# A decoder step on one core: where the first squares are made, how x and the last products are cut, and the order of the streams

## The chip, the core and the metric

The kernel runs on one NeuronCore of a Trainium2 chip. The metric is the time of one execution on the device in microseconds (us). The engines are named as in the profile: PE multiplies matrices, DVE works on vectors, ACT on scalars and activations, POOL (GpSimd) and SP (SyncE) mostly issue transfers. Each engine takes its instructions in order, and semaphores order them across engines.

## The reference

One step of a one-layer decoder with two token mixers, on 256 prompt tokens and 8 x 8 sample tokens (T = 320 columns, D = 1024). Branch A is block-sparse softmax attention with rotary queries and keys, branch B is stick-breaking attention; both read a cache of 1024 past tokens for each of the 8 samples through a page table. All is float32.

```
def decoder_layer(x, pos_start, past, w):
    h = rms_norm(x, g_mix)
    proj = einsum('btd,de->bte', h, w_in)        # q, k, v of A; q, k, v of B; two gates
    qa, ka = rope(qa, pos), rope(ka, pos)
    new_rows = (ka, va, ks, vs)                  # also outputs
    o_a = moba_block(qa, past and new keys, values)
    o_s = stick_breaking_block(qs, past and new keys, values)
    merged = (sigmoid(ga) * einsum('btw,wd->btd', o_a, w_branch_moba)
              + sigmoid(gs) * einsum('btw,wd->btd', o_s, w_branch_sb))
    x = x + einsum('btd,de->bte', merged, w_out)
    h2 = rms_norm(x, g_ffn)
    ff = silu(einsum('btd,df->btf', h2, w_ffn_gate)) * einsum('btd,df->btf', h2, w_ffn_up)
    return x + einsum('btf,fd->btd', ff, w_ffn_down), new_rows
# prompt: no past; sample: past = cache[page_table]; then y = rms_norm(x, g_final)
```

## The kernel before

Activations lie with D on the 128 partitions (8 pieces) and the 320 tokens as columns. Every matrix product is made of three: both factors are split into a high part that PE takes in its fast 32-bit form and a low part, the rest; high by high, low by high and high by low are added in one PSUM tile. A weight tile (128 x 1024, 512 KB) so costs a load on SP's queue into one of three raw buffers `wr`, a copy on ACT (`wh`), a subtraction on DVE (`wl`), both into one of three pairs of buffers, and 24 matmuls of 320 columns.

The head (`load_x`) loads x in quarters of two pieces and the first two weights in halves, makes the high and low parts `xs` and `xl` piece by piece, and squares x for the first norm: four ACT instructions of two pieces each into `sq`, and on DVE two folds and a last add. `rsqrt` then sums over the partitions with six short matmuls (`cs`) after the third dense tile, ACT and DVE turn this into `rtok`, and `first_norm` spreads it to `rstd` with the matmuls `rb` after the fourth.

The attention part interleaves six streams: dense tiles (`d`: queries and keys, values, later the branch products), scores of sample pairs against cached keys (`s`), transposed probabilities and cached values (`a`), prompt attention (`p`), ends (`e`), gates (`g`). The string `ORDER` of 113 letters gives the order of their steps; `Plan.run` takes one step for each letter and then calls `loads.feed`. A pair's scores and its values both come in two halves, and each half takes two tiles of 1 MB from a ring of 8 buffers `cr`. So the first pair (branch 0, samples 0 and 1) has the letters s s, then a a a: probabilities, first half of the values, second half.

`loads.feed` starts loads in the order of need, with at most one cache tile for each call, as long as buffers are free. Keys (`kr`) and weights go out on SP's one queue in that order. Values (`vr`) are gathered by POOL; ahead of each gather POOL copies one element of the second last key tile (`seen`), so that a gather starts only when that key tile has landed. PE, POOL and SP keep the order in which the program is written; the other engines are ordered by a scheduler after the head.

After that come the output projection, the feed-forward part and the down projection, whose PE work is dense, and `last_norm`: PE sums the squares, ACT and DVE make `r`, and the eight pieces are multiplied by it and stored, six by DVE one at a time and the last two by POOL.

## Time and profile before

| | |
|---|---|
| median of 3 runs | 558.27 us (555.37 to 559.37) |
| profiled execution | 559.79 us, its span 558.0 us |
| mean granted clock of PE | 0.993 |
| PE | 542.0 us busy, 97% of the span |
| DVE, ACT, POOL | 329.7, 269.9, 49.8 us busy |
| DMA | 138.86 MB, mean 249 GB/s |

The span is the profiled execution from its first to its last instruction. All rows below come from this one execution, so sums are made against its 559.79 us. The page divides the span into 40 slices of 14 us; PE shows 8 or 9 tenths in each but the last.

### The profile page before, as it was taken

The numbers are of one execution on the slowest core, as the hardware profiler recorded it, in microseconds if no ns is written. First come the engines' busy times: TensorE is split into PE (matmuls) and PEld (weight loads), VectorE is DVE, ScalarE is ACT, GpSimd is POOL, SyncE is SP. The second block draws the span as 40 slices with busy tenths as digits, with TensorE's granted clock in tenths as the row PEclk, the third lists the DMA queues.
The fourth block names the chain that finished last, engine by engine and source line by source line (L and its number), as shares of the span: only waits on it lengthen the run. The fifth ranks groups of instructions, "written<-read, shape, count | busy, mean of one in ns | idle before, by whom it ended". The sixth has DMA issues, their size and how long they took to land.

```text
span 558.0 us, 10927 instructions
## 1 busy us (share of the span) xinstructions
PE 542.0 (97%) x4252; PEld 493.2 (88%) x4252; DVE 329.7 (59%) x600; ACT 269.9 (48%) x484; POOL 49.8 (9%) x73
## 2 busy tenths in 40 slices
PE   8999999999999999999999999999999999999993
PEld 5888676878878678878999999999999999999992
DVE  5786655464468537763778666555556665443433
ACT  6895555436675436542445464444333333353421
POOL 0001212150034302130000000000000000000001
PEclk9899999999999999999999999999999999999998
DMA  6999999999799999995595544544445454545512
GB/s 218 369 395 395 337 378 401 401 408 403 256 348 362 419 392 333 388 373 208 171 331 158 149 148 150 150 149 151 146 147 149 144 155 134 155 145 143 169 34 94
DMA packets 45572, 138.86 MB, mean 249 GB/s; under 512 B 5201, under 2 KB 7505, under 8 KB 41297
## 3 DMA queue, kind: packets, MB, share of 16 engines
q1 hardware_dynamic: 40336, 104.06, 54.8%
q0 software_dynamic: 4608, 33.56, 14.8%
q8 instruction: 33, 0.54, 0.4%
q10 hardware_dynamic: 576, 0.56, 0.3%
q14 instruction: 19, 0.15, 0.1%
HBM read 134.22 MB, written 3.93 MB: 248 GB/s over the span
## 4 chain that ended last, share of the span: by engine, by line
PE 82%; DMA 9%; DVE 3%; ACT 2%; SPq 1%; issue 1%; POOL 1%; DVEq 0%; POOLq 0%; ACTq 0%
PE dps L185 55%; PE dps L344 15%; PE po L696 4%; DMA vr<-in_cv,small 4%; DMA kr<-in_ck 3%; PE S L571 3%; DMA wr<-in_w_in 1%; DVE wl L153 1%; SPq L533 1%; PE tp L504 1%; PE tp L672 1%; PE dps L518 1%; PE dps L388 1%; PE dps L463 1%; DMA small<-in_c_small 1%
## 5 line engine op out<-in xcount | busy, mean ns | idle before, releaser
L152 ACT ACTIVATE wh<-wr 128x1024 fp32r<-128x1024 f32 (+1 forms) x122 | 127.2, 1046 | 179.5 <-issue 104.5
L153 DVE TENSOR_TENSOR wl<-wr,wh 128x1024 fp32r<-128x1024 f32 (+1 forms) x122 | 147.0, 1206 | 67.9 <-ACT wh L152 66.9
L185 PE MATMUL dps<-x1h,wh 128*128 128x320 f32 x352 | 109.0, 310 | 0.0
L185 PE MATMUL dps<-x1l,wh 128*128 128x320 f32 x352 | 108.8, 309 | 0.0
L185 PE MATMUL dps<-x1h,wl 128*128 128x320 f32 x352 | 108.8, 309 | 0.0
L344 PE MATMUL dps<-xs,wh 128*128 128x320 f32 x256 | 78.8, 320 | 0.9 <-ACT xs L306 0.9
L344 PE MATMUL dps<-xl,wh 128*128 128x320 f32 x256 | 77.2, 314 | 0.3 <-DVE xl L307 0.3
L185 PEld LDWEIGHTS dps<-x1h,wh 128*128 128x128 f32 x352 | 66.1, 188 | 0.1
L185 PEld LDWEIGHTS dps<-x1l,wh 128*128 128x128 f32 x352 | 66.1, 188 | 0.0
L185 PEld LDWEIGHTS dps<-x1h,wl 128*128 128x128 f32 x352 | 66.1, 188 | 0.0
L185 PE MATMUL dps<-fh,wh 128*128 128x320 f32 x176 | 54.4, 309 | 0.0
L185 PE MATMUL dps<-fl,wh 128*128 128x320 f32 x176 | 54.4, 309 | 0.0
L185 PE MATMUL dps<-fh,wl 128*128 128x320 f32 x176 | 54.4, 309 | 0.0
L344 PEld LDWEIGHTS dps<-xs,wh 128*128 128x128 f32 x256 | 48.8, 191 | 4.7 <-issue 2.0
L344 PEld LDWEIGHTS dps<-xl,wh 128*128 128x128 f32 x256 | 48.9, 191 | 1.1 <-DVE xl L307 1.0
L344 PE MATMUL dps<-xs,wl 128*128 128x320 f32 x256 | 43.2, 309 | 0.0
L344 PEld LDWEIGHTS dps<-xs,wl 128*128 128x128 f32 x256 | 39.1, 188 | 0.2 <-DVE wl L312 0.2
L541 POOL DMA_INDIRECT vr<-in_cv,small x32 | 35.9, 1121 | 19.1 <-PE po L696 8.6
L696 PE MATMUL po<-vr,pt 128*32 128x256 f32 x512 | 32.1, 381 | 2.9 <-DMA vr<-in_cv,small 2.9
L185 PEld LDWEIGHTS dps<-fh,wh 128*128 128x128 f32 x176 | 33.0, 188 | 0.0
L185 PEld LDWEIGHTS dps<-fl,wh 128*128 128x128 f32 x176 | 33.0, 188 | 0.0
L185 PEld LDWEIGHTS dps<-fh,wl 128*128 128x128 f32 x176 | 33.0, 188 | 0.0
(203 smaller groups left out, 844.6 us busy)
## 6 DMA issues: line engine op xcount, KB each, us to landing
kr<-in_ck SPq DMA_DIRECT2D x128, 256.0 KB
wr<-in_w_ff SPq DMA_DIRECT2D x44, 512.0 KB
wr<-in_w_in SPq DMA_DIRECT2D x30, 512.0 KB
wr<-in_w_down SPq DMA_DIRECT2D x16, 448.0 KB
wr<-in_w_v SPq DMA_DIRECT2D x8, 512.0 KB
wr<-in_w_b SPq DMA_DIRECT2D x8, 512.0 KB
wr<-in_w_out SPq DMA_DIRECT2D x8, 512.0 KB
wr<-in_w_down SPq DMA_DIRECT2D x8, 512.0 KB
```

What stands on the lines that cost most here:

```text
L152: self.nc.scalar.activation(hi, raw, AF.Copy)
L153: self.nc.vector.tensor_tensor(lo, raw, r32(hi), ALU.subtract)
L185: nc.tensor.matmul(ps, w, x, start=first and i == 0, stop=last and i == len(todo) - 1)
L344: self.nc.tensor.matmul(ps, a, x, start=k + low + i == 0, stop=low == 1 and k + n == KD and i == n - 1)
L388: nc.tensor.matmul(ps, self.xs[:, k], w[k][j], start=k + j == 0, stop=k + j == KD)
L463: nc.tensor.matmul(S[e][:, i], q[r, 2 * u + i, half * P:half * P + P], k[r, 2 * u + i, half * P:NP_], start=True, stop=True)
L504: nc.tensor.transpose(tp[:, i * P:(i + 1) * P], src, self.ident)
L518: nc.tensor.matmul(po[r, i, :NP_ if kt else P], t["v"][:, kt, c0:c0 + HD], mv, start=kt == 1, stop=kt == 0)
L533: nc.sync.dma_start(raw[:, g], ck[bass.ds(at[g] * P, P), :])
L541: self.nc.gpsimd.indirect_dma_start(out=raw.rearrange("p a b -> p (a b)"), out_offset=None, in_=self.I[f"cv{br}"], in_offset=bass.Indirect ...
L571: nc.tensor.matmul(S[r], self.block(QS, x, hp), raw[x][:, :, hp * P:(hp + 1) * P], start=i == 0, stop=i == 1)
L696: nc.tensor.matmul(po[r], PT[j][:, r], v[:, c:c + 256], start=j == 0, stop=j == 8)
```

## The change

Five things change.

First squares: the first two pieces of x are squared right behind the second piece's high part, inside the loop over pieces, and the other three squares follow in a loop that adds each result on DVE at once, 640 columns at a time, where there was one add of 1280 and one of 640.

x lies in memory as four contiguous quarters, and the later reload of x for the residual is four transfers.

The last products: pieces 0 and 1 alone as before, then the last two on POOL, then 2 and 3, and 4 and 5, together on DVE; five stores in place of seven, on SP, ACT, ACT, SP, SP.

`ORDER` and `FIRST` have new letters: the second half of the first pair's values comes ahead of the third pair's first scores, the two halves of values of several pairs stand side by side, and gates move. `feed` counts with a variable that equals `self.ready` for `WLAG = 0`. `queries` of the second branch's first pair are made one step group earlier.

```
@@ -36,7 +36,9 @@
 
 LAG = 2
 PACE = 1
-FIRST = "wwwwc"
+
+WLAG = 0
+FIRST = "wwwcww"
 ORDERED = {mybir.EngineType.PE, mybir.EngineType.Pool, mybir.EngineType.SP}
 STARTED = ORDERED | {mybir.EngineType.DVE, mybir.EngineType.Activation}
 WR, WB = 3, 3
@@ -50,8 +52,8 @@
 
 
 ORDER = (
-    "dddddddsdddsdddsdaspaddsadasegaddaapedsapdpsggdaapepaaddgpds"
-    "spepdgddpsagasapggegapaapgpsseggpggpdsagdasaaedgaaded"
+    "dddddddsdddsdddsdasaddpasadsedpdgaaadspdpseggdaaapegpaaddpds"
+    "spepddgdpsaggsaapggegapaappsseggpggpdsagdasaaedgaaded"
 )
 
 
@@ -94,14 +96,17 @@
 
     def feed(self):
 
+        ready = self.ready
         while self.raw and self.ready - self.used["w"] < WB:
             self.split_one()
+        if not WLAG:
+            ready = self.ready
         left, held, begun = [], set(), 0
         for kind, load in self.todo:
             if kind == "c":
                 free = self.begun["c"] - self.used["c"] < RB and begun < PACE
             else:
-                free = self.begun["w"] - self.ready < WR
+                free = self.begun["w"] - ready < WR
             if free and kind not in held:
                 tile = load()
                 (self.raw if kind == "w" else self.got["c"]).append(tile)
@@ -289,7 +294,7 @@
         w = [self.wpool.tile([P, 1024], F32, name=self.uid("wr"), tag="wr", bufs=WR) for i in range(2)]
         parts = [self.weight_parts() for i in range(2)]
         load_w = lambda i, h: nc.sync.dma_start(w[i][:, half[h]], self.I["w_in"][i][:, 4 * h:4 * h + 4])
-        load_x = lambda g: nc.sync.dma_start(x[:, 2 * g:2 * g + 2], self.I["x"][:, 2 * g:2 * g + 2])
+        load_x = lambda g: nc.sync.dma_start(x[:, 2 * g:2 * g + 2], self.I["x"][g])
         nc.scalar.dma_start(self.small, self.I["c_small"])
         for h in range(2):
             load_x(2 * h)
@@ -310,13 +315,14 @@
             if k % 4 == 1:
                 for (hi, lo), raw in zip(parts, w):
                     nc.vector.tensor_tensor(lo[:, half[h]], raw[:, half[h]], r32(hi[:, half[h]]), ALU.subtract)
+            if k == 1:
+                nc.scalar.activation(sq[:, 0:2], x[:, 0:2], AF.Square)
         self.loads.are_split(parts)
         self.loads.split_one()
-        for k in range(0, KD, 2):
+        for k in range(2, KD, 2):
             nc.scalar.activation(sq[:, k:k + 2], x[:, k:k + 2], AF.Square)
+            nc.vector.tensor_add(sq[:, :2], sq[:, :2], sq[:, k:k + 2])
         nc.scalar.activation(self.xs[:, :, NS:], r32(self.xl[:, :, NP_:]), AF.Copy)
-        for n in (4, 2):
-            nc.vector.tensor_add(sq[:, :n], sq[:, :n], sq[:, n:2 * n])
         self.sq = self.stg.tile([P, T], F32, name="sq", tag="y", bufs=3)
         nc.vector.tensor_add(self.sq, sq[:, 0], sq[:, 1])
 
@@ -418,10 +424,11 @@
                 self.first_norm()
             while todo:
                 self.qk_tile(br, *todo.pop(0))
-            if f == HP - 1:
+            if f % 8 == HP - 1:
 
                 for u in range(2):
-                    self.queries(br, u)
+                    if br == 0 or f"s0{u + 2}" in self.plan.done:
+                        self.queries(br, u)
 
     def gen_v(self, br):
         for c in range(2):
@@ -765,7 +772,8 @@
         self.x1h = xh = q.tile([P, KD, T], F32R, name="x1h")
         self.x1l = xl = q.tile([P, KD, T], F32R, name="x1l")
         self.rstd2 = rstd = q.tile([P, T], F32, name="rstd2")
-        nc.sync.dma_start(x1, I["x"])
+        for g in range(4):
+            nc.sync.dma_start(x1[:, 2 * g:2 * g + 2], I["x"][g])
         acc = self.acc1 = q.tile([P, 1, T], F32, name="acc1")
         def part(e, k0, k1):
             w, ps = made[e]
@@ -856,13 +864,11 @@
 
         rb = self.pp.tile([P, T], F32, name="rstd3", tag="s", bufs=SB)
         nc.scalar.activation(rb, r, AF.Copy)
-        e = 0
-        for i, n in enumerate((1, 1, 1, 1, 1, 1, 2)):
-            s = slice(e, e + n)
-            engine, v = (nc.gpsimd, r) if i == 6 else (nc.vector, rb if i else r)
-            engine.tensor_tensor(x1[:, s], xg[:, s], v[:, None, :].to_broadcast([P, n, T]), ALU.mult)
-            (nc.scalar if i % 2 else nc.sync).dma_start(self.O["y"][:, s], x1[:, s])
-            e += n
+        tiles = (nc.vector, nc.sync, 0, 1), (nc.vector, nc.scalar, 1, 2), (nc.gpsimd, nc.scalar, 6, 8), (nc.vector, nc.sync, 2, 4), (nc.vector, nc.sync, 4, 6)
+        for engine, queue, e0, e1 in tiles:
+            v = r if engine is nc.gpsimd or e0 == 0 else rb
+            engine.tensor_tensor(x1[:, e0:e1], xg[:, e0:e1], v[:, None, :].to_broadcast([P, e1 - e0, T]), ALU.mult)
+            queue.dma_start(self.O["y"][:, e0:e1], x1[:, e0:e1])
 
     def needs(self):
 
@@ -967,7 +973,7 @@
     f = lambda x: np.ascontiguousarray(x)
     xp, xs = np.asarray(i["x_prompt"]), np.asarray(i["x_sample"])
     x = np.concatenate([xp[0, ::-1], xs[:, ::-1].reshape(NS, D)])
-    a["x"] = f(x.T.reshape(KD, P, T).transpose(1, 0, 2))
+    a["x"] = f(x.T.reshape(4, 2, P, T).transpose(0, 2, 1, 3))
 
     def tiles(w, k, n):
         return f(np.asarray(w).reshape(k, P, n, P).transpose(2, 1, 0, 3))
```

The order of instructions, first on ACT at the head, before (`sq` are the squares, `wh_151` and `wh_258` the high parts of the third and fourth weight):

```order
L309 ACTIVATE wh_111<-wr_108 128x512
L306 ACTIVATE xs<-x_105,small 128x320 x3
L309 ACTIVATE wh_109<-wr_107 128x512
L306 ACTIVATE xs<-x_105,small 128x320
L309 ACTIVATE wh_111<-wr_108 128x512
L306 ACTIVATE xs<-x_105,small 128x320 x2
L152 ACTIVATE wh_151<-wr_122 128x1024
L316 ACTIVATE sq_106<-x_105 128x640 x4
L317 ACTIVATE xs<-xl 128x8x64
L152 ACTIVATE wh_258<-wr_124 128x1024
```

The squares stand together there, ahead of `wh_258`. After, on ACT at the same place:

```order
L314 ACTIVATE wh_111<-wr_108 128x512
L319 ACTIVATE sq_106<-x_105 128x640
L311 ACTIVATE xs<-x_105,small 128x320 x3
L314 ACTIVATE wh_109<-wr_107 128x512
L311 ACTIVATE xs<-x_105,small 128x320
L314 ACTIVATE wh_111<-wr_108 128x512
L311 ACTIVATE xs<-x_105,small 128x320 x2
L157 ACTIVATE wh_152<-wr_122 128x1024
L323 ACTIVATE sq_106<-x_105 128x640 x3
L325 ACTIVATE xs<-xl 128x8x64
L157 ACTIVATE wh_261<-wr_124 128x1024
```

One of the four squares has moved up between the first high parts of the weights. On DVE at the head, before (`wl` are low parts of weights, the `sq` rows are the adds):

```order
L312 TENSOR_TENSOR wl_112<-wr_108,wh_111 128x512
L307 SCALAR_TENSOR_TENSOR xl<-x_105,small,xs 128x320 x2
L153 TENSOR_TENSOR wl_152<-wr_122,wh_151 128x1024
L319 TENSOR_TENSOR sq_106<-sq_106 128x1280
L153 TENSOR_TENSOR wl_259<-wr_124,wh_258 128x1024
L319 TENSOR_TENSOR sq_106<-sq_106 128x640
L321 TENSOR_TENSOR sq<-sq_106 128x320
```

The add of 1280 columns is ahead of the fourth weight's low part and the one of 640 behind it. After, on DVE:

```order
L317 TENSOR_TENSOR wl_112<-wr_108,wh_111 128x512
L312 SCALAR_TENSOR_TENSOR xl<-x_105,small,xs 128x320 x2
L158 TENSOR_TENSOR wl_153<-wr_122,wh_152 128x1024
L324 TENSOR_TENSOR sq_106<-sq_106 128x640 x3
L158 TENSOR_TENSOR wl_262<-wr_124,wh_261 128x1024
L327 TENSOR_TENSOR sq<-sq_106 128x320
```

All three adds of 640 now stand ahead of that low part, and the last add is right behind it. On POOL, the gathers of the first pair's values (the first three `vr`; `seen` reads the key tile that it waits for), before:

```order
L541 DMA vr_616<-in_cv,small 128x2048
L540 COPY seen<-kr_536 1x1
L541 DMA vr_656<-in_cv,small 128x2048
L540 COPY seen<-kr_768 1x1
L541 DMA vr_893<-in_cv,small 128x2048
```

The gather `vr_893`, for the second half of those values, stands behind key tile `kr_768`, the first of the third pair. After, on POOL:

```order
L548 DMA vr_617<-in_cv,small 128x2048
L547 COPY seen<-kr_537 1x1
L548 DMA vr_657<-in_cv,small 128x2048
L547 COPY seen<-kr_537 1x1
L548 DMA vr_769<-in_cv,small 128x2048
```

That gather, now `vr_769`, waits for the same key tile as the two before it. On SP's queue, from the ninth dense tile's weight on, before:

```order
L157 DMA wr_601<-in_w_in 128x1024
L157 DMA wr_659<-in_w_in 128x1024
L157 DMA wr_695<-in_w_in 128x1024
L157 DMA wr_697<-in_w_in 128x1024
L529 TENSOR_LOAD small
L533 ISA
L533 DMA kr_768<-in_ck 128x512
```

Four weights go out ahead of `kr_768`, keys for the third pair. After, on SP:

```order
L162 DMA wr_602<-in_w_in 128x1024
L162 DMA wr_660<-in_w_in 128x1024
L162 DMA wr_696<-in_w_in 128x1024
L162 DMA wr_698<-in_w_in 128x1024
L162 DMA wr_829<-in_w_in 128x1024
L162 DMA wr_831<-in_w_in 128x1024
L536 TENSOR_LOAD small
L540 ISA
L540 DMA kr_872<-in_ck 128x512
```

Six weights stand ahead of that pair's keys, now `kr_872`, and the two that were behind them have moved up.

## Rows read from the trace of the kernel before

**Rows 1.** the page's busy times: engine, us, share of the span, instructions

```profile
PE 542.0 (97%) x4252; PEld 493.2 (88%) x4252; DVE 329.7 (59%) x600; ACT 269.9 (48%) x484; POOL 49.8 (9%) x73
```

**Rows 2.** waits of PE: line, awaited engine and tile; us, times, longest

```profile
PE po L696 <- DMA vr<-in_cv,small: 2.9, 3, 1.3
```

**Rows 3.** timeline of ACT at the head: start, length, line, tiles; idle before

```profile
8.59 1.47 ACT L306 ACTIVATE xs<-x,small 128x320 fp32r<-128x320 f32 x3 [2.00 <-DMA x<-in_x]
...
13.64 2.61 ACT L316 ACTIVATE sq<-x 128x640 f32<-128x640 f32 x4
...
16.68 1.05 ACT L152 ACTIVATE wh<-wr 128x1024 fp32r<-128x1024 f32 x1
```

**Rows 4.** timeline of DVE at the head

```profile
13.77 1.23 DVE L153 TENSOR_TENSOR wl<-wr,wh 128x1024 fp32r<-128x1024 f32 x1
...
16.28 1.49 DVE L319 TENSOR_TENSOR sq<-sq 128x1280 f32<-128x1280 f32 x1 [1.28 <-ACT sq L316]
...
18.90 0.82 DVE L319 TENSOR_TENSOR sq<-sq 128x640 f32<-128x640 f32 x1
...
19.75 0.49 DVE L321 TENSOR_TENSOR sq<-sq 128x320 f32<-128x320 f32 x1
...
25.32 0.16 DVE L267 SCALAR_TENSOR_TENSOR rtok<-nw,rtok 128x3 f32<-128x3 f32 x1
```

**Rows 5.** timeline of PE at the head

```profile
20.30 0.83 PE L261 MATMUL cs<-ones,sq 128*128 128x1 f32 x6 [1.33 <-DVE sq L321]
```

**Rows 6.** windows: busy time by engine, then granted PE clock, DMA share, GB/s

```profile
21.58:24.99 3.41, 3.41 (x15) 3.41 (x14) 2.57 (x5) 1.98 (x3) 0.00 (x0) 0.50 1.01 359
...
93.86:100.00 6.14, 6.13 (x57) 5.20 (x58) 0.78 (x4) 3.55 (x7) 2.29 (x4) 1.00 1.01 408
```

**Rows 7.** chain of waits, the fourth and a later tile of 24 matmuls

```profile
21.13 5.16 PE dps L344 x24
...
107.46 3.52 PE dps L344 x24
```

**Rows 8.** timeline of PE, scores and values of the middle

```profile
76.12 1.92 PE L571 MATMUL S<-kr,QS 128*32 128x512 f32 x16
...
79.08 1.71 PE L696 MATMUL po<-vr,pt 128*32 128x256 f32 x26 [0.62 <-DMA vr<-in_cv,small]
...
93.86 1.92 PE L696 MATMUL po<-vr,pt 128*32 128x256 f32 x28 [1.33 <-DMA vr<-in_cv,small]
...
186.85 1.50 PE L696 MATMUL po<-vr,pt 128*32 128x256 f32 x24 [0.96 <-DMA vr<-in_cv,small]
```

**Rows 9.** timeline of POOL, the copy that waits for a key tile

```profile
64.90 0.18 POOL L540 COPY seen<-kr 1x1 f32<-1x1 f32 x1 [13.24 <-DMA kr<-in_ck]
```

**Rows 10.** timeline of SP's queue, loads in the order of issue

```profile
58.12 5.04 SPq L533 DMA_DIRECT2D kr<-in_ck  x8
...
64.68 2.48 SPq L157 DMA_DIRECT2D wr<-in_w_in  x2
...
68.44 7.46 SPq L533 DMA_DIRECT2D kr<-in_ck  x8
```

**Rows 11.** chain of waits, from the last issue to the landing

```profile
71.58 9.48 DMA kr<-in_ck
...
83.23 10.59 DMA vr<-in_cv,small
```

**Rows 12.** windows in the first half, columns as in group 6

```profile
44.00:58.00 14.00, 13.95 (x132) 12.40 (x131) 8.07 (x20) 7.52 (x20) 2.48 (x4) 1.00 1.03 390
...
58.00:76.00 18.00, 18.00 (x171) 13.66 (x169) 11.64 (x34) 10.32 (x32) 3.23 (x4) 1.00 0.95 341
```

**Rows 13.** timeline of DVE and windows at the end

```profile
551.86 2.08 DVE L863 TENSOR_TENSOR x<-xg,rstd 128x320 f32<-128x320 f32 x5
...
553.50:555.50 2.00, 0.00 (x0) 0.00 (x0) 0.43 (x2) 0.00 (x0) 0.00 (x0) 0.64 1.00 357
...
555.50:556.00 0.50, 0.00 (x0) 0.00 (x0) 0.00 (x0) 0.00 (x0) 0.00 (x0) 0.50 1.06 412
```

More of the change, by code (lines that the diff above doesn't have):

```diff
@@ L38 @@
 PACE = 1
-FIRST = "wwwwc"
+WLAG = 0
+FIRST = "wwwcww"
 ORDERED = {mybir.EngineType.PE, mybir.EngineType.Pool, mybir.EngineType.SP}
@@ L52 @@
 ORDER = (
-    "dddddddsdddsdddsdaspaddsadasegaddaapedsapdpsggdaapepaaddgpds"
-    "spepdgddpsagasapggegapaapgpsseggpggpdsagdasaaedgaaded"
+    "dddddddsdddsdddsdasaddpasadsedpdgaaadspdpseggdaaapegpaaddpds"
+    "spepddgdpsaggsaapggegapaappsseggpggpdsagdasaaedgaaded"
 )
@@ L95, in feed @@
     def feed(self):
+        ready = self.ready
         while self.raw and self.ready - self.used["w"] < WB:
             self.split_one()
+        if not WLAG:
+            ready = self.ready
         left, held, begun = [], set(), 0
@@ L103, in feed @@
             else:
-                free = self.begun["w"] - self.ready < WR
+                free = self.begun["w"] - ready < WR
             if free and kind not in held:
@@ L312, in load_x @@
                     nc.vector.tensor_tensor(lo[:, half[h]], raw[:, half[h]], r32(hi[:, half[h]]), ALU.subtract)
+            if k == 1:
+                nc.scalar.activation(sq[:, 0:2], x[:, 0:2], AF.Square)
         self.loads.are_split(parts)
         self.loads.split_one()
-        for k in range(0, KD, 2):
+        for k in range(2, KD, 2):
             nc.scalar.activation(sq[:, k:k + 2], x[:, k:k + 2], AF.Square)
+            nc.vector.tensor_add(sq[:, :2], sq[:, :2], sq[:, k:k + 2])
         nc.scalar.activation(self.xs[:, :, NS:], r32(self.xl[:, :, NP_:]), AF.Copy)
-        for n in (4, 2):
-            nc.vector.tensor_add(sq[:, :n], sq[:, :n], sq[:, n:2 * n])
         self.sq = self.stg.tile([P, T], F32, name="sq", tag="y", bufs=3)
@@ L420, in gen_qk @@
                 self.qk_tile(br, *todo.pop(0))
-            if f == HP - 1:
+            if f % 8 == HP - 1:
                 for u in range(2):
-                    self.queries(br, u)
+                    if br == 0 or f"s0{u + 2}" in self.plan.done:
+                        self.queries(br, u)
     def gen_v(self, br):
@@ L767, in out_proj @@
         self.rstd2 = rstd = q.tile([P, T], F32, name="rstd2")
-        nc.sync.dma_start(x1, I["x"])
+        for g in range(4):
+            nc.sync.dma_start(x1[:, 2 * g:2 * g + 2], I["x"][g])
         acc = self.acc1 = q.tile([P, 1, T], F32, name="acc1")
@@ L858, in last_norm @@
         nc.scalar.activation(rb, r, AF.Copy)
-        e = 0
-        for i, n in enumerate((1, 1, 1, 1, 1, 1, 2)):
-            s = slice(e, e + n)
-            engine, v = (nc.gpsimd, r) if i == 6 else (nc.vector, rb if i else r)
-            engine.tensor_tensor(x1[:, s], xg[:, s], v[:, None, :].to_broadcast([P, n, T]), ALU.mult)
-            (nc.scalar if i % 2 else nc.sync).dma_start(self.O["y"][:, s], x1[:, s])
-            e += n
+        tiles = (nc.vector, nc.sync, 0, 1), (nc.vector, nc.scalar, 1, 2), (nc.gpsimd, nc.scalar, 6, 8), (nc.vector, nc.sync, 2, 4), (nc.vector, nc.sync, 4, 6)
+        for engine, queue, e0, e1 in tiles:
+            v = r if engine is nc.gpsimd or e0 == 0 else rb
+            engine.tensor_tensor(x1[:, e0:e1], xg[:, e0:e1], v[:, None, :].to_broadcast([P, e1 - e0, T]), ALU.mult)
+            queue.dma_start(self.O["y"][:, e0:e1], x1[:, e0:e1])
     def needs(self):
```

4 lines of the change are left out of this document (2 added, 2 removed).

## The prediction

> **What bounds the kernel now.** I read the page's first part, then the waits of TensorE (PE), then the timeline and the chain of waits around each of them. PE is busy for 542.0 of 558.0 us [rows 1], so an edit can win only what PE idles or loses in slow matmuls. Its waits are few: 2.9 us in three waits for gathered values [rows 2] and 1.33 us for the first squares [rows 5]. What follows 551.86 us is products and stores with PE done [rows 13]. Of the other engines' work only what lies under a PE wait, or in that tail, counts.
>
> [...]
>
> **The first squares (head).** Before, the four squares run in a row on ScalarE (ACT), 2.61 us from 13.64, and the high part `wh` of the next weights ends at 17.73 [rows 3]. VectorE (DVE) then has an add of 1.49 us, the low part of those weights, an add of 0.82 us and one of 0.49 us, ending at 20.24 [rows 4]; `cs` starts at 20.30. After, the first square moves into a stretch in which ACT sat 2.00 us waiting for x [rows 3], so its 0.65 us (a quarter of 2.61) costs nothing there if the third quarter of x comes no earlier than now. ACT then reaches `wh` 0.65 us sooner, at about 16.05, and ends it at 17.1. On DVE three adds of 640 columns (0.82 us each at most) replace 1280 and 640. They alternate with the squares and are done by about 17.4. The low part (1.23 us) follows, to 18.6, and the last add of 0.49 us ends near 19.1. PE is free at 20.30 − 1.33 = 18.97. So the idle falls from 1.33 to about 0.2 us: **−1.1 us**.
>
> Would the clock still fall? An idle of the same 1.33 us at 93.86 is followed by 1.00 throughout [rows 6, 8], so such a gap doesn't drop it every time; the one at the head comes after only some 10 us of PE work. I take the drop to hang on the gap and count 5.16 − 3.52 = **−1.64 us**, between 0 and −1.64. [...]
>
> Against it: `rstd` comes from `cs` by a short chain on ACT and DVE that ended with `rtok` at 25.48 [rows 4], 4.35 us after `cs` (21.13). Beside a tile of 3.52 us at full clock up to 0.8 us of it could show before `rb`. Its first step stood behind two low parts on DVE, which now start sooner; I take +0.2. The head sums to −1.1 − 1.6 + 0.2 = **−2.5 us**.
>
> On SyncE (SP), which issues loads strictly in order, the first key load now stands ahead of the seventh weight. One key tile is 1 MB, at 390 GB/s [rows 12] 2.7 us. That weight is used two tiles, or 7 us, after the first `rb`: covered, and about 2 us of cover is left.
>
> **The new order (middle).** All three value waits have one shape: a gather is issued late, because POOL's `seen` copy waits for a key tile, and lands 9 to 11 us later. The gathers of the last half of the first pair stood behind `seen` at 64.90 [rows 9] and PE waited 0.62 us at 79.08; those of the second pair were issued at 83.23 and took 10.59 us [rows 11], and PE waited 1.33 us at 93.86; a later one cost 0.96 us at 186.85 [rows 8]. In the new order the first of these looks at a key tile that is loaded one pair earlier (the POOL rows above), and some 14 us of notice become over 20. Between the scores of the pair and the second, two dense tiles of 3.52 us and a prompt step come in, over 7 us; ahead of the third, one tile, 3.52 us. Each is more than its wait. That takes away **−2.9 us** of idle time.
>
> What is late next: the keys that now follow the moved values, `kr_872` and the tile after it. Six weight loads stand ahead of them on SP, not four, and the last two issue only when DVE has freed a buffer (64.68 to 67.16 [rows 10]). The keys so start where the next pair's did, 68.44. Eight issues took 5.04 us in one stretch and 7.46 in the next [rows 10]; by the first they end at 73.5. The tile issued from 58.12 was seen at 64.90 [rows 9, 10], which is about 4.5 us after its half of the issues: landing near 78. PE gets there at 76.12 plus the moved values (some 2.3 us for a second half): 78.4 [rows 8]. Both sides move 2.5 us earlier with the head, as the free buffer hangs on PE. The slack is about nothing. Bytes allow it: DMA moved 341 GB/s from 58 to 76 us against 390 before that [rows 12], so 0.9 MB, 2.2 us of transfer, are unused there. With the longest landing of a key that the chain shows, 9.48 us [rows 11], the wait would be 9.48 − 4.5 = 5 us. I take +0.4 here, nearer to the first since the gathers that stretched the second have gone from that stretch, and +0.4 for the two joined pairs of values further on, whose four gathers of 1 MB need 11 us at 390 GB/s, beside two weights and a key tile (5 us more), in some 20 us: from the landing of the key that they wait for, near 81, to 93.86 plus the 7. Both together reach from 0 to +5.
>
> Middle: −2.9 + 0.8 = **−2.1 us** (−2.9 to +2).
>
> **Edits at nothing.** x as contiguous quarters moves the same bytes at the same places of the queue, and each partition's part of a quarter is 2560 bytes as before; what it could give is bounded by the 2.00 us that ACT idles for x [rows 3], what it could cost by as much; I keep ±0.5, as most of what ACT waits for is there before PE needs it. The reload of x as four loads adds three issues on SP where the next weight waits for a free buffer anyway. Making the second branch's first queries early moves two copies to DVE and ACT; PE waits for neither now. The new counter in `feed` changes nothing, since with `WLAG` 0 it reads the value that it read before.
>
> **The tail.** Now the last five products end at 551.86 + 2.08 = 553.94, and stores drain at 357 GB/s while packets are of one tile and at 412 when they are of the pair [rows 13]. In pairs DVE ends at the same time (the same columns), the pair of POOL goes ahead of the last two, and six eighths of 1.31 MB go at 412: 0.98/412 + 0.33/357 is 3.3 us, against 3.7 at 357. But the last store begins only at 553.94 with 0.33 MB still to move. I take **−0.2 us** (−0.5 to +0.5). [...] The rows speak for a queue that is full there, not for one transfer by itself.
>
> **Sum.** −2.5 − 2.1 − 0.2 = −4.8 against the profiled execution: 559.79 − 4.8 = 555.0. That execution lies 1.5 us above the median of the three runs (558.27), so I forecast 553.5 for the median.
>
> **Rivals.**
> (a) The clock falls anyway, at the same or another place: +1.6, thus 555.1. For it: a gap of the same size decides once and not another time [rows 6, 8]. Against it: no other drop stands in the middle. Chance 0.2.
> (b) Supply binds: PE arrives 2.5 us sooner from the head, but transfers run near their rate already [rows 12], so it waits for the same bytes. The head's gain is spent by the first late key, and the rest is the order's: 553.5 + 2.5 = 556.0, up to 557.3 if the longest value wait, 1.33, remains too; then the change doesn't do what it says. For it: the 390 GB/s. Against it: the 2.2 us left unused. Chance 0.2.
> (c) Slower: the six weights ahead make both key tiles of that pair land like the slowest, 9.48 us [rows 11], at each half: 2 × 5 us less the 0.8 already counted, 562.7. It is slower from the point at which these waits pass 0.8 + 4.8 = 5.6 us together. Against it: nothing but these keys then moves. Chance 0.07.
> (d) All goes as hoped: no new wait, clock kept, stores −0.5: 552.4, and 551 if the gaps' restarts (a value wait shows about 0.2 us more by the matmuls' pitch) count too. Chance 0.15.
> The forecast itself, 552 to 555, has 0.38.
>
> **How the numbers follow.** The range must cover (a), (b), (d) and the spread of runs (555.37 to 559.37 for the same kernel): 549.8 to 558.0. One per cent, about what a measurement here can tell from no change, puts the bounds at 552.7 and 563.9. Faster by over 1%: (d) and about half of the forecast's band, 0.35. Within 1%: 0.60. Slower: the far end of (c), 0.05.
>
> **What would show it.** `cs` with under 0.4 us of idle; no granted 0.50 between 20 and 30 us; no wait for `vr` in 70 to 190 us; a wait of under 1 us, if any, before the scores near 76 us; the last product at about 549, last packet 2.3 us later. Wrong would be a wait for `kr` of several us, or a granted clock of 0.50 in a new place.

## The result, and the profile after

The changed kernel takes 560.51 us (median of 11 runs, 558.69 to 563.75), the kernel before 557.37 beside it (11 runs, 555.37 to 559.37): ratio 1.0057, 95% interval 1.0036 to 1.0077. It is slower by 0.6%, where 0.9% less was forecast (553.5 against 558.27); 553.5 was 7 us too low, and the time lies outside the range. Two slow runs, one of e5 (594.11 us at a granted clock of 0.849) and one of the kernel before (886.41 at 0.558), are left out of all figures below.

The profiled execution after is the median one: 560.51 us, span 558.7, granted clock 0.994. That of before was 559.79, which turned out 1.6 to 2.8 us above the medians of its later runs (557.0 to 558.2). So the two traces differ by only 0.7 us in time, and a second trace of before is set beside them below.

The waits of PE after (line, awaited engine and tile; us, times, longest):

```profile
PE dps L350 <- DVE qT L370: 1.7, 1, 1.7
PE dps L350 <- ACT wh L314: 1.1, 1, 1.1
...
PE po L703 <- DMA vr<-in_cv,small: 0.8, 1, 0.8
PE S L578 <- ACT QS L609: 0.5, 1, 0.5
...
PE S L578 <- DMA kr<-in_ck: 0.5, 2, 0.3
PE tp L511 <- ACT oT L723: 0.3, 1, 0.3
```

Both waits that the change was forecast to remove are shorter: values 2.9 us [rows 2] to 0.8, first squares 1.33 [rows 5] to 0.17. But the whole list sums to 7.3 us in 13 waits, against 7.0 in 10 before. Others took their place: the first rotated queries `qT`, the keys, `oT`.

The head after, on PE (start, length, line, tiles; idle before and its releaser):

```profile
19.01 0.83 PE L266 MATMUL cs<-ones,sq 128*128 128x1 f32 x6 [0.17 <-DVE sq L327]
23.72 1.04 PE L280 MATMUL rb<-ident,rtok 128*128 128x128 f32 x6 [0.25 <-PE dps L350]
30.23 0.39 PE L350 MATMUL dps<-xs,wh 128*128 128x320 f32 x1 [1.75 <-DVE qT L370]
38.04 2.13 PE L578 MATMUL S<-kr,QS 128*32 128x512 f32 x16 [0.54 <-ACT QS L609]
```

The column sums come 1.29 us earlier than in [rows 5], and `rb` 2.41 us earlier, so that at `rb` nearly all of the 2.5 us is there that the forecast had for the head. By the first scores nothing of it is left: they start at 38.04. `rb` and the first scores before:

```profile
26.13 0.97 PE L275 MATMUL rb<-ident,rtok 128*128 128x128 f32 x6
37.78 1.92 PE L571 MATMUL S<-kr,QS 128*32 128x512 f32 x16
```

ACT and DVE after show where it went:

```profile
24.47 1.06 ACT L157 ACTIVATE wh<-wr 128x1024 fp32r<-128x1024 f32 x1 [2.57 <-DMA wr<-in_w_in]
25.56 0.21 ACT L421 ACTIVATE rtok<-rtok 64x1 f32<-64x1 f32 x1
26.16 1.06 ACT L157 ACTIVATE wh<-wr 128x1024 fp32r<-128x1024 f32 x1 [0.39 <-DMA wr<-in_w_in]
27.12 0.42 ACT L331 ACTIVATE rstd<-rb 128x320 f32<-128x320 f32 x1
```

```profile
25.57 1.22 DVE L158 TENSOR_TENSOR wl<-wr,wh 128x1024 fp32r<-128x1024 f32 x1 [1.95 <-ACT wh L157]
27.25 1.22 DVE L158 TENSOR_TENSOR wl<-wr,wh 128x1024 fp32r<-128x1024 f32 x1 [0.46 <-ACT wh L157]
28.39 0.48 DVE L334 TENSOR_TENSOR turn<-turn,rstd 128x320 f32<-128x320 f32 x1
```

The splits of two weights stand ahead of `rstd` on ACT and of `turn` on DVE, and both weights come late. Counted by the loads in the trace they are the sixth, which the key tile overtook on SP (the prediction and the expectations count it as the seventh), and the seventh, which was behind that tile before, too. Before, the sixth was there in time:

```profile
21.29 2.00 ACT L152 ACTIVATE wh<-wr 128x1024 fp32r<-128x1024 f32 x2
```

The middle, SP's queue after:

```profile
46.41 23.04 SPq L162 DMA_DIRECT2D wr<-in_w_in  x6
70.61 11.19 SPq L540 DMA_DIRECT2D kr<-in_ck  x16
```

Six weight loads take 23 us to issue, and the keys start at 70.61, where [rows 10] had them from 58.12 and the forecast 68.44. SP's waits from 46 to 72 us, after, are nearly all for DVE to free a raw buffer (21 us of the 26; before it was 12.0):

```profile
SPq L162 <- DVE wl L158: 6.7, 2, 5.7
SPq L162 <- DVE st L648: 6.6, 1, 6.6
SPq L162 <- DVE st L646: 4.0, 1, 4.0
SPq L162 <- DVE pown L636: 3.5, 1, 3.5
```

And in that time DMA has little or nothing to do. Windows after (last column GB/s):

```profile
60.00:64.00 4.00, 4.00 (x39) 2.88 (x28) 2.88 (x5) 1.79 (x3) 0.00 (x0) 1.00 1.01 420
64.00:68.00 4.00, 4.00 (x68) 1.74 (x66) 3.65 (x11) 1.91 (x3) 0.00 (x0) 1.00 0.54 216
68.00:72.00 4.00, 4.00 (x31) 3.97 (x28) 2.31 (x8) 1.60 (x7) 0.00 (x0) 1.00 0.40 126
...
58.00:76.00 18.00, 18.00 (x172) 13.90 (x172) 11.75 (x29) 10.42 (x26) 0.00 (x0) 1.00 0.75 278
```

Over 58 to 76 us that is 278 GB/s for the 341 of [rows 12]: 1.1 MB less, 2.9 us of transfer at 390. The keys are late by it. PE feels that at the third pair's scores:

```profile
78.52 1.03 PE L578 MATMUL S<-kr,QS 128*32 128x512 f32 x4
79.75 1.91 PE L578 MATMUL S<-kr,QS 128*32 128x512 f32 x12 [0.21 <-DMA kr<-in_ck]
```

These sixteen matmuls take 3.14 us, from 78.52 to 81.66, where sixteen took 1.92 before [rows 8]. The list of waits names 0.2 of these 1.2 us, since the end of a matmul is modelled in the profile (592 ns for one of these, at a pitch of 120 in the row of 1.92 us) and can cover a part of the gap behind it. The gathers that look at the keys are late too: POOL sees the third of that pair's four key tiles at

```profile
82.57 0.30 POOL L547 COPY seen<-kr 1x1 f32<-1x1 f32 x1 [28.10 <-DMA kr<-in_ck]
```

From the second norm on, nothing differs. Its `rb` after, and that of before:

```profile
325.45 0.97 PE L280 MATMUL rb<-ident,rtok 128*128 128x128 f32 x6
```

```profile
324.71 0.97 PE L275 MATMUL rb<-ident,rtok 128*128 128x128 f32 x6
```

From there to the end of the span both take 233.3 us. So what differs is made in the first 325 us.

### The profile page after: what moved, and what is told of

It is laid out like the page before. It is cut to its first block, busy times and chain, and to the rows that moved or that the text cites. A ratio compares the mean times of both kernels' runs of the same rounds, so it can differ in the third digit from the quotient of the medians.

```text
span 558.7 us, 10940 instructions
## 1 busy us (share of the span) xinstructions
PE 542.4 (97%) x4252; PEld 491.6 (88%) x4252; DVE 330.3 (59%) x599; ACT 272.0 (49%) x486; POOL 47.7 (9%) x73
## 4 chain that ended last, share of the span: by engine, by line
PE 84%; DMA 7%; DVE 4%; ACT 2%; issue 1%; SPq 1%; DVEq 0%; ACTq 0%
PE dps L190 56%; PE dps L350 13%; PE S L578 5%; PE po L703 4%; DMA vr<-in_cv,small 3%; DMA wr<-in_w_in 2%; DMA kr<-in_ck 2%; PE dps L394 1%; PE tp L679 1%; ACT rot L369 1%; PE dps L525 1%; PE tp L511 1%; SPq L540 1%; DVE kp L589 1%; PE dps L470 1%
## 5 line engine op out<-in xcount | busy, mean ns | idle before, releaser
L350 PE MATMUL dps<-xl,wh 128*128 128x320 f32 x256 | 75.9, 310 | 0.1
L578 PE MATMUL S<-kr,QS 128*32 128x512 f32 x256 | 34.6, 596 | 1.2 <-ACT QS L609 0.5
L548 POOL DMA_INDIRECT vr<-in_cv,small x32 | 32.5, 1016 | 30.2 <-PE tp L671 8.7
```

The source lines that it names most:

```text
L350: self.nc.tensor.matmul(ps, a, x, start=k + low + i == 0, stop=low == 1 and k + n == KD and i == n - 1)
L548: self.nc.gpsimd.indirect_dma_start(out=raw.rearrange("p a b -> p (a b)"), out_offset=None, in_=self.I[f"cv{br}"], in_offset=bass.Indirect ...
L578: nc.tensor.matmul(S[r], self.block(QS, x, hp), raw[x][:, :, hp * P:(hp + 1) * P], start=i == 0, stop=i == 1)
```

## The experiments

**The theories.** A: SP's one queue is the cause. A weight load that waits for its raw buffer holds key loads that are free to go; DMA idles, and PE, POOL's gathers and all behind them come late. At the head the same thing holds in ACT's queue: `rstd` stands behind a weight that has not landed. B: the order of the streams costs by itself, through late values or the other engines' order. C: the squares or the tail cost something.

In the table "keys from" is the time at which SP starts the key loads behind the weights that begin near 46 us (`kr` rows as above), "GB/s" is DMA's rate from 56 to 72 us, "to scores" the time from the issue of the fourth weight's load (the first `wr` row on SP after 8 us, at 12.23 in the changed kernel) to the first scores, all from the profiled execution; ratios are to runs of before on the same chip. The rows stand in the order of the rate.

| kernel | us (runs) | ratio, 95% interval | keys from | GB/s | to scores |
|---|---|---|---|---|---|
| e13 before, keys late | 566.29 (5) | 1.0153, 1.0129 to 1.0177 | 66.53 | 209 | 24.96 |
| e1 after, old opening | 562.90 (6) | 1.0080, 1.0055 to 1.0105 | 71.73 | 236 | 25.83 |
| e3 new order alone | 567.55 (6) | 1.0156, 1.0130 to 1.0182 | 73.25 | 259 | 26.11 |
| e8 after, old order | 561.06 (6) | 1.0063, 1.0040 to 1.0086 | 64.64 | 263 | 29.19 |
| e2 squares alone | 560.65 (12) | 1.0051, 1.0034 to 1.0067 | 62.66 | 266 | 26.49 |
| after | 560.51 (11) | 1.0057, 1.0036 to 1.0077 | 70.61 | 294 | 25.81 |
| e12 after, lag | 569.85 (5) | 1.0199, 1.0171 to 1.0227 | 77.70 | 307 | 27.53 |
| e11 before, lag | 558.10 (12) | 1.0002, 0.9983 to 1.0021 | 56.86 | 338 | 25.44 |
| e10 head in program order | 563.83 (4) | 1.0112, 1.0086 to 1.0138 | 59.15 | 338 | 28.62 |
| before (second trace, e4) | 559.00 (1) | | 58.09 | 343 | 26.32 |
| e9 the same, with squares | 564.90 (4) | 1.0121, 1.0095 to 1.0148 | 60.23 | 347 | 27.94 |
| e7 before, keys first | 556.45 (12) | 0.9986, 0.9972 to 1.0000 | 54.70 | 351 | 25.45 |
| e16 x and tail alone | 557.71 (12) | 1.0008, 0.9995 to 1.0022 | 58.17 | 359 | 25.95 |
| e6 squares, keys first | 557.37 (12) | 1.0003, 0.9990 to 1.0016 | 55.43 | 361 | 25.93 |
| e5 after, keys first | 558.10 (11) | 1.0015, 0.9996 to 1.0035 | 62.89 | 375 | 27.07 |
| e15 e5, old opening | 556.78 (12) | 0.9992, 0.9981 to 1.0003 | 60.59 | 392 | 24.80 |
| e14 new order, keys first | 558.93 (12) | 1.0022, 1.0006 to 1.0038 | 60.84 | 401 | 26.00 |

Every kernel under 310 GB/s there is at least 0.5% slower than before. Every one over 330 is within 0.25% of it, save e9 and e10, which carry a wait of their own. The rate tells which kernels lose but does not rank how much: e12 and e3 lose most, at 307 and 259.

In the traces, before and e13, before and e7, and e2 and e6 have the same order of instructions on ACT, DVE and POOL and differ in SP's order alone. In after against e5, and e3 against e14, the scheduler also moved a weight's split and a few softmax steps on ACT and DVE, from about 74 us on.

**Parts of the change.** e1 takes the opening back in the changed kernel, e8 the order; e2 and e3 put the squares, or the order, alone into the kernel before; e4 is the kernel before once more, for a second trace.

```
-FIRST = "wwwcww"        # e1; e8: the old ORDER in the changed kernel
+FIRST = "wwwwc"         # e2: the loop of squares alone; e3: the new ORDER alone
```

e1: 

> The changed kernel with only the old start of the loads: both weights again ahead of the first key tile. In the changed kernel the seventh weight lands at 24.45 us, ACT waits 2.57 us for it, and the copy of rtok and then rstd (27.12 us, as before the change) stand behind it on ACT. Theory 1 (that queue position ate the head's gain): rstd comes near 25 us, the 1.75 us wait of PE for qT goes, the first scores start near 36 us instead of 38.0, and what is won stays: about 558.5 us against 560.5. Theory 2 (the middle is bound by the bytes that DMA brings): the first scores start near 36 us too, but the first late key or value takes it back, and the time stays at 560 to 561. Theory 3 (the late weight is late for want of bytes, not of queue position): rstd stays at 27 us.

e2: 

> The kernel before with the first squares alone as in the change. Theory 1: cs waits under 0.3 us, the first scores start 1 to 2.6 us earlier than 37.8, and the time falls by as much against the kernel before. Theory 2: the first scores are as early, but the three waits for values grow by the same sum (2.9 us to 4 or 5), and the time is within 0.5 us of the kernel before.

e3: 

> The kernel before with the new order of the streams alone. The order moved the waits from values to keys in the profile of the changed kernel (the three waits of 2.9 us are one of 0.8, but the scores of the third pair, and of two later ones, are each longer by 0.9 to 1.3 us). Theory 2: no gain, within 1 us of the kernel before. Theory 4 (the new order is what makes the changed kernel slower): 2 to 4 us slower than the kernel before. My forecast's step: 2 us faster.

e4: 

> The kernel before as it is, for a second profile: its first one was 2.4 us slower than the median of its runs. If the clock's drop at the head comes in some runs only, this profile shows no granted 0.50 between 20 and 30 us and a span near 555.5; if it always follows the 1.33 us of idle, it shows 0.50 again.

e8: 

> The changed kernel with the old order of the streams, all its other edits kept (squares, the start of the loads, x in quarters, tail). If the new order is the part that costs, this returns to the time of the kernel before, 557.5. If the order was made to fit the other edits, this is slower than the changed kernel, as the squares alone were (560.7 or more). By theory A the traces decide it: the time follows the sum of idle DMA time before 270 us, and not the edit.

No part alone gave anything back. In e1 `rstd` starts 1 us earlier than in the changed kernel (26.14 for 27.12), but the run is slower, which neither theory had. In e2 and e3 the forecast's gains are missed too; e3 was expected 2 to 4 us slower at the worst and is 9. e8 is as slow as its second case said. e3 costs most of the four; six weights stand ahead of its keys, as after. In e2 the queue has its four weights, but the scheduler put low parts of weights behind softmax steps on DVE, the buffers come free later, the keys start at 62.66 in place of 58, and PE waits 5.1 us in three waits for values. e8 shows the same: 64.64, and 3.2 us for values.

e4 shows the head of before without the low clock of [rows 6], after the same idle:

```profile
19.30 0.83 PE L261 MATMUL cs<-ones,sq 128*128 128x1 f32 x6 [1.33 <-DVE sq L321]
25.05 1.04 PE L275 MATMUL rb<-ident,rtok 128*128 128x128 f32 x6 [1.30 <-issue]
```

The granted clock there is 1.00 from 20 to 30 us, the tile ends sooner, and PE then stands 1.30 us ahead of `rb`, whose input `rtok` DVE ends at 24.95. From `cs` to `rb` it is 5.75 us in place of 5.83 before. Eight traces have the old squares and the old opening, and in all of them PE idles 1.33 to 1.36 us ahead of `cs`. Behind that idle the granted clock falls to 0.50 in four (before, e7, e11, e14) and stays at 1.00 in four (e3, e4, e13, e16). From `cs` to `rb` the first four take 5.83 us, the others 5.28 to 5.76.

**The keys of the middle first.** Two key tiles go ahead of the last two of the six weights in the changed kernel (e5), or ahead of the last of the four in the kernel before, with (e6) and without (e7) the squares. e7 and before differ in SP's order alone.

```
-                free = self.begun["w"] - ready < WR
+                free = self.begun["w"] - ready < WR and (self.begun["w"] < 16 or self.begun["c"] >= 14)   # e5; e6, e7: 15, 12
```

e5: 

> The changed kernel with one difference on SP's queue: the two key tiles for the third pair's scores go out ahead of the last two of the six weights. In the changed kernel the six weights hold the queue from 46.4 to 69.5 us, DMA falls to 216 and 126 GB/s from 64 to 72 us, and the keys are issued from 70.6. Theory A (the queue: keys stand behind weights that wait for DVE to free a raw buffer, and DMA idles meanwhile): keys issued near 60 us, no window under 300 GB/s from 56 to 72, the wait at the third pair's scores gone and the gathers behind the seen copy at 82.6 earlier; 1.5 to 3 us faster than the changed kernel, 557.5 to 559. Theory B (bytes: DMA brings all it can): time as the changed kernel, 560.5, with the waits elsewhere.

e6: 

> The kernel before with the new first squares (the run that was 2.5 us slower), and on SP's queue the third pair's two key tiles ahead of the fourth of four weights; the order on every other engine is the same as in that run. There that weight waited for a low part on DVE that the scheduler had put later, until 61 us, and DMA fell to 134 GB/s from 60 to 64. Theory A: the wait of 2.5 us for the first pair's last values goes, and the time returns to that of the kernel before or below, 557 to 558.5 against 560.7. Theory B: it stays at 560 to 561. Theory C (the squares cost at the head): it stays too, with the values on time.

e7: 

> The kernel before, and only the place of that one weight on SP's queue changed as in the run beside it. Theory A: the gathers of the first pair's last values start some 3 us earlier, the waits of 0.6 and 1.3 us for values go or shrink, 1 to 2 us faster than the kernel before, about 556.5. Theory B: no change within 0.5 us.

SP's queue in e5, and its window:

```profile
46.01 15.67 SPq L162 DMA_DIRECT2D wr<-in_w_in  x4
62.89 5.44 SPq L540 DMA_DIRECT2D kr<-in_ck  x8
```

```profile
58.00:76.00 18.00, 18.00 (x173) 13.90 (x174) 11.58 (x28) 9.53 (x25) 0.00 (x0) 1.00 0.99 375
```

The hole is gone (375 GB/s for 278), the third pair's sixteen score matmuls take 1.90 us again, and the loss falls from 0.57% to 0.15%, as theory A expected. The squares' own loss in e2 goes the same way (e6, 0.51% to 0.03%), with SP's order alone changed. e7 is 0.14% under before, between what A and B expected, and decides nothing. e6 against e7 shows no gain for the squares: 557.37 and 556.45.

**The head.** e9 and e10 are e7 with the seventh weight ahead of the first key tile, the first three steps of ACT and DVE in the program's order, and `rtok` and `rstd` copied on DVE; e9 has the squares.

```
-FIRST = "wwwwc"
+FIRST = "wwwwwc"
-        nc.scalar.activation(self.rstd, self.along(self.rtok), AF.Copy)
+        nc.vector.tensor_copy(self.rstd, self.along(self.rtok))
+        with self.tc.manual_schedule(engines=STARTED):
+            self.steps_of(ORDER[:3])
```

e9: 

> The kernel before with the first squares pair by pair, the keys of the middle ahead of the seventeenth weight (the edit of e7), and a head that can't stand behind the seventh weight: that weight ahead of the first key tile, the first three steps of ScalarE and VectorE in the order of the program, the two short copies around rstd on VectorE. It differs from e10 by the squares alone. Theory A (the squares' gain was real at the column sums and was lost behind the splitting of a late weight): the column sums wait under 0.4 us, rstd ends 24 to 25.5, the first scores start at 35 to 36.5 against 37.8 before, and the run is about 1 us under e10. Theory B (supply sets the end whatever the head does): the first scores are as early, but the end of attention is within 0.4 us of e10's. Theory C (the head is bound by the landing of the weights in any order): first scores at 37.5 or later, as before.

e10: 

> The same without the squares' edit. Theory A: the column sums wait 1.1 to 1.4 us, rstd 25 to 26.5, first scores 36.5 to 37.5, time about 1 us over e9 and near e7 (556.4) or under it. Theory B: the same time as e9 within 0.4 us though its first scores are 1 us later. Theory C: first scores at 37.5 or later in both.

Theories A and B missed. C had first scores at 37.5 or later in both, which came (40.19 and 39.83), but not as before: they are 2 us and more later than that. A high part of the next weight now stood ahead of the queries' rotation on ACT (e9):

```profile
32.41 1.06 ACT L158 ACTIVATE wh<-wr 128x1024 fp32r<-128x1024 f32 x1 [5.58 <-DMA wr<-in_w_in]
```

and the first scores waited 4.45 us (e9) and 3.11 (e10) for `QS`. The pair does not settle what the squares are worth; it repeats in a new place that a weight which has not landed holds what follows on ACT.

**A lag of one step for weights.** `feed` counts the weights before the split, so a weight goes out one step later.

```
-WLAG = 0
+WLAG = 1                # e12; e11: the same count in the kernel before
```

e11: 

> The kernel before, each weight load issued one step of the order later, so that SyncE stands less behind a weight whose buffer isn't free and later keys go ahead of it. Theory A (a weight that waits at the head of SyncE's queue holds ready keys): the six-weight stretch shrinks, no window of 4 us between 46 and 78 us moves under 300 GB/s, 556 to 557.5 us. Rival (the weights then come late for PE): waits of the dense tiles for wh of 1 us and more, 559 or more.

e12: 

> The changed kernel with the same lag of one step, its own WLAG = 1. Theory A: the windows from 64 to 72 us move over 300 GB/s, not 216 and 126, no wait for keys over 0.5 us, and 2 us are given back: 558 to 559. Rival (the order's cost lies in the late gathers and in ScalarE's and VectorE's order, not in SyncE's queue): 560 or more, with waits for wh in the dense tiles.

e11 is as before, which neither of its cases had. e12 went the other way than expected, since the lag moves all weights and left six of them together:

```profile
47.86 28.65 SPq L162 DMA_DIRECT2D wr<-in_w_in  x6
77.70 6.48 SPq L540 DMA_DIRECT2D kr<-in_ck  x9
```

As a remedy it failed; the rival's 560 or more came, but with waits for keys and not for `wh`. As a larger dose it agrees with A: the row of weights 5.6 us longer, the keys 7.1 us later, 18 GB/s from 72 to 78 us, waits of 5.2 us for keys, and 1.99% over before in place of 0.57%. The order on ACT and DVE changed too, and the granted clock fell to 0.50 behind the waits (83 to 90 us), so the size is not the queue's alone.

**The queue alone, and the rest.** e13 is the kernel before with two key tiles held until the weights are out: six weights ahead of sixteen key loads as after, and no other engine's order changed. e14 is e3, and e15 is e1, with the hold of e5. e16 has x by quarters and the tail alone.

```
-                free = self.begun["c"] - self.used["c"] < RB and begun < PACE
+                free = self.begun["c"] - self.used["c"] < RB and begun < PACE and (self.begun["c"] < 10 or self.begun["w"] >= 17)   # e13
```

e13: 

> The kernel before with one change in SyncE's order alone: the ninth and tenth gathered key tiles of the middle wait until the eighteenth weight load has been issued, so that six weight loads stand ahead of sixteen key loads, as in the changed kernel; no other engine has another order. Theory A (a weight that waits at the head of SyncE's queue for its buffer holds ready keys, DMA idles and the time is lost there): the keys are issued at 68 to 73 in place of 58, DMA moves under 250 GB/s from 64 to 72 us in place of 337, the first value gather comes after 80, and the run is 3 us or more over before, since this order of scores has less slack than the new one: 561 to 566. Rival (keys come early enough anyhow; the changed kernel is slower by the other engines' order): within 1 us of before, 557 to 558.5.

e14: 

> The kernel before with the new order of the streams alone (as e3, 567.6) and the hold of e5: two key tiles go ahead of the seventeenth and eighteenth weight. Theory A: the stall of e3 goes, keys issued near 62, DMA over 300 GB/s in every window from 56 to 72 us, and 8 us or more are given back: 557 to 559, no better than e7 (556.4). Rival (the order costs by itself, late values or the other engines' order): 562 or more.

e15: 

> The changed kernel with the hold of e5 and the old opening order of loads, seven weights ahead of the first key tile: against e5 (558.2) it differs by the opening alone. Theory A (the head is bound by the landing of the sixth and seventh weight; the key tile ahead of them takes the squares' gain): rstd ends at 26.2 or earlier against 27.1, the wait for the first rotated queries falls from 2.1 to 1.4 or less, and the run is 0.5 to 1.5 us under e5. Rival (the opening makes no difference, as the end is set by the middle): within 0.4 us of e5.

e16: 

> The kernel before with x laid down and loaded by quarters and the last products and stores in pairs, nothing else. By both theories no difference: 557 to 558.5, and 6.5 to 6.7 us from the first of the last products to the end of the span. [...]

e13, SP's queue, DMA's rate, and PE:

```profile
45.58 19.77 SPq L157 DMA_DIRECT2D wr<-in_w_in  x6
66.53 11.73 SPq L533 DMA_DIRECT2D kr<-in_ck  x16
```

```profile
60.00:64.00 4.00, 4.00 (x44) 2.64 (x47) 3.15 (x7) 3.19 (x4) 0.00 (x0) 1.00 0.05 18
```

```profile
76.44 1.91 PE L571 MATMUL S<-kr,QS 128*32 128x512 f32 x12 [1.06 <-DMA kr<-in_ck]
83.25 1.07 PE L696 MATMUL po<-vr,pt 128*32 128x256 f32 x4 [4.90 <-DMA vr<-in_cv,small]
86.32 3.20 PE L696 MATMUL po<-vr,pt 128*32 128x256 f32 x26 [2.00 <-DMA vr<-in_cv,small]
```

The queue's order by itself costs 1.5%, with DMA at 18 GB/s for 4 us. The price is paid mostly at the values, whose gathers wait for the late key tile, not at the keys. A part of it is the clock: the granted clock is 0.50 from 81 to 91 us, behind these waits, and the last 26 matmuls take 3.20 us where [rows 8] has 1.71. In e14 the loss of e3 falls from 1.56% to 0.22%. Theory B, as the main cause, falls with these two: e13 has no new order of streams, and e14 has it and is 0.22% from before. Of B is left that e14's 0.22% is clear of noise (1.0006 to 1.0038), and that e14 is 0.36% above e7, which has the old order and keys first too; e15, with the new order and the other edits, shows no such loss (0.9992).

e15 against e5 has the opening alone edited: 0.0023 by the ratios, 1.3 us, hardly more than their intervals leave open. In the traces of e5, e8 and e12 the granted clock falls to 0.50 behind the wait for `qT` (in e5 from 30.5 to 34 us), in e15 and after it doesn't, so a part of the 1.3 us may be the clock. ACT in e15 waits for one weight ahead of `rstd`, not two:

```profile
24.18 1.06 ACT L157 ACTIVATE wh<-wr 128x1024 fp32r<-128x1024 f32 x1 [2.25 <-DMA wr<-in_w_in]
25.26 0.20 ACT L421 ACTIVATE rtok<-rtok 64x1 f32<-64x1 f32 x1
25.37 0.42 ACT L331 ACTIVATE rstd<-rb 128x320 f32<-128x320 f32 x1
```

e16 differs from before by nothing that its interval excludes; from the first of the last products (550.51) to the end of its span it is 6.6 us. It and e14 and e15 came out as theory A expected, and e13 too, 0.3 us over its range and with the hole earlier, from 60 to 64 us.

## Why the prediction was wrong

**What the loss is made of.** From after to e5 the ratio falls by 0.0042 (the queue in the middle), from e5 to e15 by 0.0023 (the opening), and e15 lies 0.0008 under before. In us at 557 that is 2.3 + 1.3 − 0.4 = 3.2; these steps lead from after to before, so they add up to the whole by construction. By the intervals the first is known to about 1.6 us and the second to about 1.2, so the first is clear of noise and the second is at its edge. The parts don't add in any order: with the queue in the way, the old opening was no help (e1). e15 keeps all the other edits, the early queries of the second branch among them, and is not slower than before.

**"The slack is about nothing ... I take +0.4" is the step that failed.** The prediction saw the six weights ahead of the keys and the wait for DVE's buffer, and priced the result by the keys' landing alone. Two things were missed. The last weight issues stand behind DVE's softmax work, so the keys began at 70.61, not at 68.44 less the 2.5 us of the head. And while SP waits there DMA has next to nothing to move (4 GB/s from 68 to 70 us): the 2.2 us of transfer left unused before became 216 and 126 GB/s in two windows, and all keys and gathers after that inherit the delay. For the +0.4 at these keys the trace has 1.2 us (78.52 to 81.66), and behind it 0.8 for the values at 103.58 and a wait for keys at 215. Rival (c) had the six weights and the sign, at a chance of 0.07, but another mechanism: keys that land slowly, in 9.48 us. They landed 3.7 to 5.1 us after their issue; it was the issue that came late, and waits of over 5.6 us at those keys were not needed.

**The covered weight of the opening.** "That weight is used two tiles after the first `rb`: covered" counted PE's use. ACT and DVE split the weight long before that, and `rstd` and `turn` stand behind the split. That order is in the traces; its price, 1.3 us in e15 against e5, is at the edge of the noise. In the four kernels with the new opening PE waits 1.7 to 3.0 us for `qT`, in the twelve with the old one (e9 and e10 left out) at most 0.8; from the fourth weight's load to the first scores it is 27.4 us on average against 25.7. But after itself, where the clock stays at 1.00, has 25.8; the three with 0.50 behind that wait have 27.1 to 29.2.

**−1.1 us for the squares.** The size was right and the worth nothing. From the fourth weight's load to `cs` it is 7.94 to 7.98 us in the eight kernels of those twelve without the new squares and 6.79 to 6.83 in the four with them: 1.15 us. From the same load to `rstd` both take 14.9 on average, and without and with them 25.7 and 25.8 to the first scores. In all four with the squares `rstd` on ACT follows the split of a weight that ACT waited for as it landed, and the squares don't move that landing. Of the eight without them four have the same; in before, e7 and e11, three of the four with 0.50 there, `rstd` waits for `rb`.

**−1.64 us for the clock, +0.2 for the chain to `rtok`.** After, the granted clock is 1.00 from 12 to 94 us and the wait ahead of `rb` is 0.25 us, both as forecast against that one trace. What was wrong is to take the 1.64 us, the difference of [rows 7] beside the 0.50 of [rows 6], as a cost of the kernel before. Four of the eight traces with that head have no 0.50, and there `rb` comes only 0.07 to 0.55 us sooner after `cs`, since PE then waits for `rtok`; up to `rb`, that is all the drop costs. Rival (a) has come true elsewhere: e1, e2, e5, e8 and e12 have the new squares and 0.50 at 25 to 36 us, behind another wait. What decides whether the clock falls is not shown: behind the same idle of 1.33 to 1.36 us four of the eight traces have 0.50 and four have 1.00.

**−2.9 us for the values.** After, 0.8 of them is left, in e15 none. But with the transfers as full as they are (392 GB/s) the waits moved: e15 has 1.51 us for keys at 154.85 and 1.25 for `oT` at 221.60, neither of which stands among the waits of before. For the keys that looks like rival (b), PE waiting for the same bytes elsewhere; no run tests it. The value waits also vary between traces of the same order: 2.9, 2.5 (e4) and 1.9 (e16). The forecast counted from the largest.

**−0.2 us for the tail; edits at nothing.** From the first of the last products to the end it is 6.6 us in both. The quarters of x: nothing in e16 that its interval excludes. The 0.2 us were an estimate from the rates of [rows 13]; no run shows them, nor a later end: e16 has 6.6 us too.

**The base.** The sum was made against an execution that lies over 1.6 us above the kernel's median, and the 1.5 us were taken as a constant. Its head began late: the fourth weight's load went out at

```profile
12.35 0.33 SPq L157 DMA_DIRECT2D wr<-in_w_in  x1
```

and in the fifteen other traces of the table but e9 and e10 at 10.79 to 12.23, 11.4 on average. And it had the largest value waits of the three, which the sum then took off in full.

**Left open.** Why the head begins up to 1.6 us later in one execution than in another is not shown. That the scheduler's order makes e2 and e8 slow was read from their traces; e6 supports it for e2, and no kernel had the squares with the other engines' order kept. Whether the opening costs anything by itself, and what the new order costs with keys first (e14), is not settled.

The best kernel measured is e7, the kernel before with two key tiles ahead of one weight: 0.14% under before, at the edge of its interval (0.9972 to 1.0000).

## What to carry to other kernels

On a queue that issues in order, look not only at what stands ahead of a load, but at what each of these waits for. In e13 weight loads without a buffer, ahead of key loads with one, left DMA at 18 GB/s from 60 to 64 us, and the price appeared later, at work that names another tile: 4.90 us of wait for values at 83.25. To judge a changed order, compare the rate of DMA in windows of 4 us between the traces; the hole showed there before PE waited for it, in e13 from 60 us where the first such wait ends at 76.44, in the changed kernel from 64 us and 79.75. Compare the length of whole rows of matmuls too: in the changed kernel the list of waits names 0.2 us where sixteen matmuls take 1.2 us longer.

The cover of a load ended here where its first reader on any engine stood, with everything queued behind that reader, and not at the matmul that uses it: in the changed kernel ACT waited 2.57 us for a weight ahead of `rstd`, and PE later 1.75 us for `qT`. And a gap on PE was worth only what was left of it at the next place where PE waited for something that the gap doesn't move: the new squares bring `cs` 1.15 us closer to the fourth weight's load and leave the first scores at 25.8 us from it, against 25.7.

## What the runs showed that was not expected

A drop of the granted clock to 0.50 for 3.4 us, with 24 matmuls in 5.16 us in place of 3.52, cost 0.07 to 0.55 us net, since the next input was late anyway. The same idle left the clock at 1.00 in another execution of the same kernel (e4), and in three kernels with the same head (e3, e13, e16).

Between 64 and 72 us the changed kernel moved 171 GB/s on average while PE was busy throughout (8.00 of 8.00 us), and none of PE's waits in that stretch names it. The two late weight loads hold an engine that mostly waits there (SP, 21 of the 26 us from 46 to 72): in e13 two weight loads put ahead of eight key loads changed the time by 1.5%.
